# Hybrid attention and gated-MLP block: early gate weights, a second fill bank, and PSUM banks that take a second product

## The chip, the cores and the metric

The kernel runs on one core of a Trainium2 chip. Its time is device microseconds of one execution, the median of several runs. Beside the runs there is one profiled execution with a trace of every engine: PE (TensorE), DVE (VectorE), ACT (ScalarE), POOL (GpSimd) and the queues that issue transfers (SP).

## The reference, cut to what matters

```python
h = rmsnorm(x, norm_gain)                                   # x: 1024 tokens x 1024
q, k, v, gate_a, u_in, v_in, gate_b, g_merge = split(h @ w_in)
attn = block_attention(rope(norm(q)), rope(norm(k)), v) * silu(gate_a)   # 8 q heads, 2 kv heads, 64 wide
y_a  = attn @ w_proj_attn                                   # 512 -> 1024
vv   = layernorm(gelu(v_in))
gm   = gelu(u_in) * (W_s vv + b) * silu(gate_b)             # mixing inside 128-token chunks
y_b  = gm @ w_proj_gmlp                                     # 512 -> 1024
g    = sigmoid(g_merge + b_merge)                           # 1024 tokens x 2 branches x 1024
y    = g[..., 0, :] * y_a + g[..., 1, :] * y_b
out  = rmsnorm(x + y @ w_out, final_gain)
```

Everything is float32. `g_merge` is the widest product: 1024 tokens by 1024 inputs by 2048 outputs.

## The kernel before, in words

Each float32 operand of a matmul is split into a high and a low part (`split`, `split16`), and each product runs as three matmuls: high by high, high by low, low by high (`mm3`). ACT makes the high part, and DVE mostly the low one. The work stands on chip transposed, with channels on the partitions and tokens along the free axis, in halves of 512 tokens.

The program runs through these stages:

- projections of k, v and q (0 to about 138 us);
- attention (about 138 to 437 us). `scores` makes a block of 128 queries by 1024 keys and its softmax, a transposing DMA turns the result, and `mix` multiplies it by v. Between the blocks run the "fills": the projections of u_in, gate_a and gate_b, each a 512 by 512 block of 24 matmuls (`z_mm`) named u20, u21, ga00 and so on;
- `proj_b` makes y_b in eight steps yb0 to yb7 (389 to 447 us). Between them `x_chunk` makes the operands of the gates on DVE and ACT (`make_forms`, the tiles named xf);
- eight gate pairs g0 to g7 (`pair`), with four pairs of y_a products between them (`proj_pair`, named y00 to y03), 456 to 653 us. Each goes through `seven`, which multiplies two 2 x 2 block matrices with seven products instead of eight, and adds the products up on DVE. The products are called 11, 21, T2, T3, T1, 22 and T4; each is 12 matmuls for a gate and 6 for y_a;
- the output projection (`out_mm`, 653 to 735 us) and the final norm.

For a gate pair `pair_weights` loads two weight tiles (`graw`), squares them on ACT for a scale (`gsq`, written to a throw-away tile in the mix's PSUM bank), sums over the partitions with a small matmul (`usg`, in the fill bank), makes the scale with DVE and POOL (`scg`, lines 671 to 675), and forms three sums of weights (`sums`: s1, s2 and a new a21). `pair` then splits each of the seven weights with that scale (`split16`, lines 680 and 681; `wg011` is the weight of product 11 of g0). `MORDER` is the order in which the program writes the gate stage down.

Two kinds of storage matter for the change. PSUM has eight banks of 128 x 512 float32: three tiles `S` of two banks each, one bank `o` (the mix, and the squares' throw-away output) and one bank `z` (the fills and `usg`). In SBUF the tag `t2` has four buffers of 128 x 512. From these come the weight sums s1 and s2 of each gate, the copy `p1` of product 11, the sums `ps` of y_a, and the work tiles of the fills.

The order on each engine is not the one in which the code is written: the program is built with a scheduler that reorders all of it by its own estimate of a timeline. Each engine then works its queue strictly in order, with semaphore waits where a tile is needed or has to come free. A wait goes by tile, so that for a two-bank tile of PSUM it does not tell its banks apart.

Of the kernel before, what the change touches and what calls it, by code (L numbers as in the profile page):

```python
# [12 lines left out]
AF = mybir.ActivationFunctionType  # L13
# [17 lines left out]
def hybrid_block_kernel(  # L31
# [11 lines left out]
    act, dve, pool, pe = nc.scalar, nc.vector, nc.gpsimd, nc.tensor  # L43
# [27 lines left out]
    def ps_s(name):  # L71
        return ps.tile([P, 1024], F32, tag="S", bufs=3, name=name)
# [10 lines left out]
    def H(h):  # L83
        return slice(512 * h, 512 * h + 512)

    def C(c):
        return slice(128 * c, 128 * c + 128)
# [80 lines left out]
        nc.sync.dma_start(out=xn, in_=x[C(tt), :])  # L168
        act.activation(xn, xn, AF.Square, accum_out=ssx[:, tt:tt + 1])

    def mm3(o, ah, al, bh, bl, start, stop):
        pe.matmul(o, ah, bh, start=start, stop=False)  # L172
        pe.matmul(o, ah, bl, start=False, stop=False)  # L173
        pe.matmul(o, al, bh, start=False, stop=stop)  # L174

    kvs = [ps_s(f"kv{b}") for b in range(2)]
    kvb = [s[:, H(h)] for s in kvs for h in range(2)]
    for i in range(4):
        for j in range(2):
            dt = 2 * i + j  # L180
# [4 lines left out]
            raw = load_x(dt)  # L185
# [6 lines left out]
            for tt in range(NT):  # L192
                o = kvb[tt // 2][:, 256 * (tt % 2):256 * (tt % 2) + 256]
# [50 lines left out]
    bmh = const([P, 16], "bmh")  # L244
# [10 lines left out]
    for h in range(2):  # L255
        raw = sb.tile([P, 512], F32, tag="wraw", bufs=4, name=f"wspr{h}")
# [177 lines left out]
    for t2k in range(4):  # L434
# [5 lines left out]
        for v in range(2):  # L440
            for half in range(2):
                dst = kT[64 * half:64 * half + 64, 2 * v:2 * v + 2, 256 * t2k:256 * t2k + 256]
# [54 lines left out]
        dve.scalar_tensor_tensor(out=t, in0=t, scalar=1.0, in1=w, op0=ALU.add, op1=ALU.mult)  # L497
        return t

    FB = (ps_z,)  # L500
    nfill = []

    def fill_bank(name):
# [181 lines left out]

    def seven(name, n, w, B, c, weights):

        def product(key, raw):
            hi, lo = weights(key, raw)
            bank = ps_s(f"{name}{key}")[:, H(0)]  # L690
            for j in range(n):
                mm3(bank, hi[:, C(j)], lo[:, C(j)], *B[key][j], j == 0, j == n - 1)
            return bank

        def add(dst, bank, other):
            dve.tensor_tensor(out=dst, in0=bank, in1=other, op=ALU.add)

        a11, a12, a21, a22, s1, s2 = w
        p1 = t2(f"p1{name}")
        act.copy(p1, product("11", a11))  # L700
        add(c[0][0], product("21", a12), p1)
        add(c[0][1], product("T2", s2), p1)
        dve.tensor_tensor(out=s2, in0=a12, in1=s2, op=ALU.subtract)
        add(c[1][0], product("T3", a21), c[0][1])
        o = product("T1", s1)
        add(c[1][1], o, c[1][0])
        add(c[0][1], o, c[0][1])
        add(c[0][1], product("22", s2), c[0][1])
        yield
        add(c[1][0], product("T4", a22), c[1][0])  # L710
        yield

    def sums(a11, a12, a21, a22, s1, s2):
# [19 lines left out]
    XLO = (dve, dve)  # L733
    XCS = (0, 1, 3, 5)
    EARLY = 2
    MORDER = "w0 g0 w1 g1 w2 A a0 g2 w3 g3 w4 a1 g4 w5 g5 w6 a2 g6 w7 a3 o g7"

    gk = []

# [12 lines left out]
    def load_chunk(j):  # L752
        for dt in (j, j + 4):
            xraw[dt] = t4(XT[j], f"xraw{dt}")
            nc.sync.dma_start(out=xraw[dt], in_=xT[C(dt), :])

    def x_chunk(j):
        q = {}
        for r in range(2):
            dt = j + 4 * r  # L760
            for h in range(2):
                t = q[r, h] = xraw[dt][:, None, H(h)]
                dve.scalar_tensor_tensor(out=xraw[dt][:, H(h)], in0=xraw[dt][:, H(h)], scalar=gs[:, dt:dt + 1],
                                         in1=rB[:, H(h)], op0=ALU.mult, op1=ALU.mult)

        def xf_tile(key, i):
            if not xfn:
                tag = XFT.pop(0)
                if tag == "ptr":
                    t = sb.tile([P, 4, 2, 1, 512], F16, tag="ptr", bufs=2, name=f"xf{key}{j}")  # L770
                else:
                    t = t4(tag, f"xf{key}{j}", F16, (P, 2048)).rearrange("p (n f k t) -> p n f k t", n=2, f=2, k=1)
                xfn.extend(t[:, n] for n in range(t.shape[1]))
            t = xfn.pop(0)
            return t[:, 0], t[:, 1]

        make_forms(q, 1, xf_tile, XB, XSUB, XHI, XLO)

    for j in range(2):
        load_chunk(j)  # L780
    for dt in range(8):
        proj_b(dt)
        if dt in XCS:
            j = XCS.index(dt)
            x_chunk(j)
            if j + 2 < 4:
                load_chunk(j + 2)

    def halves_of(t):
        return [t[:, H(0)], t[:, H(1)]]  # L790

    def proj_pair(i, b, G, dst):
        r0, r1 = load_w(W_PROJ + 2 * i, b), load_w(W_PROJ + 2 * i + 1, b)
        s12 = t2(f"ps{b}{i}")
        w = sums(r0[:, 0:256], r0[:, 256:512], r1[:, 0:256], r1[:, 256:512], s12[:, 0:256], s12[:, 256:512])
        count = [0]

        def weights(key, raw):
            t = sb.tile([P, 2, 256], F32R, tag="wh", bufs=WHB, name=f"wp{b}{i}{key}")
            split(t[:, 0], t[:, 1], raw, act, WPL[count[0] % len(WPL)])  # L800
            count[0] += 1
            return t[:, 0], t[:, 1]

        for _ in seven(f"y{b}{i}", 2, w, G, [halves_of(d) for d in dst], weights):
            pass

    def pair_weights(dt):
        t = t8("qT", 4, f"graw{dt}", F32)
        nc.sync.dma_start(out=t[:, 0, :], in_=wall[W_TR + 20 + dt])
        nc.sync.dma_start(out=t[:, 1, :], in_=wall[W_TR + 12 + dt])  # L810
        a21, a22, a11, a12 = (t[:, k, H(h)] for k in range(2) for h in range(2))
        ss = small(f"gss{dt}", 4)
        for i, t in enumerate((a21, a22, a11, a12)):
            act.activation(junk(f"gsq{dt}{i}"), t, AF.Square, accum_out=ss[:, i:i + 1])
        sc = unit_scale(ss, 4, f"g{dt}")
        return sums(a11, a12, a21, a22, t2(f"s1{dt}"), t2(f"s2{dt}")), sc

    def pair(dt, w, sc):
        def weights(key, raw):
            t = sb.tile([P, 2, 512], F16, tag="wl", bufs=3, name=f"wg{dt}{key}")  # L820
            split16(t[:, 0], t[:, 1], raw, sc, GPW)
            return t[:, 0], t[:, 1]

        ga, gb = (t4(GGT.pop(0), f"g{k}{dt}") for k in "ab")
        it = seven(f"g{dt}", 4, w, XB, [halves_of(ga), halves_of(gb)], weights)
        next(it)
        act.activation(ga, ga, AF.Tanh, bias=bmh[:, dt:dt + 1], scale=sc[:, 1:2])
        next(it)
        act.activation(gb, gb, AF.Tanh, bias=bmh[:, 8 + dt:9 + dt], scale=sc[:, 1:2])
        return ga, gb  # L830

    GGT = GGTAGS.split() * 16
# [4 lines left out]
        dve.tensor_tensor(out=ys[dt], in0=ys[dt], in1=ga, op=ALU.add)  # L837

    gates, GA, pws, yas = {}, {}, {}, {}
    yhl, who = {}, []  # L840

    wor, who4 = [], []
# [39 lines left out]
    for step in MORDER.split():  # L882
        i = int(step[1:] or 0)
# [149 lines left out]
```

## Time and profile before

| what | value |
|---|---|
| runs | 746.56, 747.24, 745.75 us (median 746.56) |
| profiled execution, own time | 744.79 us |
| its span, first to last instruction | 743.0 us |
| mean granted TensorE clock | 0.988 |
| busy: PE, DVE, ACT, POOL | 712.1, 596.4, 446.8, 97.2 us |

The profiled execution is 1.77 us under the median, and its own time is 1.79 us longer than its span. Times of day below, such as 456 us, count from the start of that span. A row of a timeline gives start, duration, engine, line, operation, output<-inputs, and in square brackets the idle time ahead of it with what ended that. Durations of pipelined instructions overlap, so the cost of one in a dense stretch is the distance between two starts. In a table by stretch the columns are the stretch and its length, and then the busy time (with the number of instructions) of PE, weight load, DVE, ACT and POOL, the granted clock, the share of the DMA engines and GB/s.

### The profile page before, as it was taken

Reading aid. Unit: us, or ns where it says so; the run is one execution under the profiler, and the core shown is the slowest. Engines: PE = TensorE matmul, PEld = TensorE weight load, DVE = VectorE, ACT = ScalarE, POOL = GpSimd, SP = SyncE. Lnnn points to the kernel's source line nnn. Section 1 sums busy time; section 2 is a strip of 40 time slices with the busy share of each in tenths; the row PEclk is TensorE's granted clock in tenths of the full one; section 3 lists DMA queues with packets and bytes.
Section 4 is the critical chain, followed back from the end, with each engine's and each line's share of the span. In section 5 each row is a group of like instructions: output and inputs, shape, how many; then the busy total and the mean of one; then the engine's idle time right before and its main releaser. Section 6 shows DMA issues by size and latency. Waiting matters only on the chain.

```text
span 743.0 us, 9814 instructions
## 1 busy us (share of the span) xinstructions
PE 712.1 (96%) x3561; PEld 530.1 (71%) x3561; DVE 596.4 (80%) x931; ACT 446.8 (60%) x775; POOL 97.2 (13%) x77
## 2 busy tenths in 40 slices
PE   8999999988999999999999995999999998999995
PEld 8978888766778888888878882455464555588884
DVE  5568988789798999988899999899888899934223
ACT  6646664676788898768787488555474446611101
POOL 0010242142121321232200002000000000000000
PEclk9999999989999999999999998999999999999998
DMA  8831301083769897898999800130031006241111
GB/s 309 301 100 36 114 15 42 1 142 78 136 128 181 166 179 142 162 177 157 166 234 323 183 16 1 56 128 15 18 125 57 0 1 231 109 142 68 46 58 56
DMA packets 152609, 85.47 MB, mean 115 GB/s; under 512 B 135408, under 2 KB 136048, under 8 KB 152560
## 3 DMA queue, kind: packets, MB, share of 16 engines
q1 hardware_dynamic: 152272, 84.56, 45.7%
q8 instruction: 28, 0.46, 0.3%
q10 hardware_dynamic: 288, 0.28, 0.1%
q14 instruction: 21, 0.17, 0.1%
HBM read 47.07 MB, written 4.19 MB: 69 GB/s over the span
## 4 chain that ended last, share of the span: by engine, by line
PE 81%; DVE 9%; DMA 4%; ACT 2%; issue 2%; POOL 1%; SPq 0%; POOLq 0%; DVEq 0%; ACTq 0%
PE o L575 6%; PE out L174 4%; PE out L173 4%; PE out L172 4%; DMA T<-p 3%; PE s L550 3%; PE s L551 3%; PE g L172 3%; PE g L174 3%; PE g L173 3%; PE q L172 2%; PE q L174 2%; PE v L172 2%; PE q L173 2%; PE v L173 2%; PE v L174 2%
## 5 line engine op out<-in xcount | busy, mean ns | idle before, releaser
L564 DVE SCALAR_TENSOR_TENSOR p<-P,ri,p 128x1024 f16<-128x1024 f32 x64 | 88.9, 1393 | 14.7 <-ACT p L563 14.3
L557 ACT ACTIVATE P<-s,nm 128x1024 f32<-128x1024 f32 x64 | 71.4, 1116 | 23.0 <-DVE nm L553 11.5
L553 DVE TENSOR_REDUCE nm<-s 128x1 f32<-128x1024 f32 x64 | 77.8, 1215 | 5.7 <-PE s L551 5.4
L563 ACT ACTIVATE p<-P,ri 128x1024 f16<-128x1024 f32 x64 | 72.8, 1143 | 14.7 <-DMA T<-p 11.3
L575 PE MATMUL o<-T,vS 128*128 128x256 f16 x512 | 61.8, 273 | 2.1 <-DMA T<-p 2.1
L575 PEld LDWEIGHTS <-vS 128*128 128x128 f16 x512 | 47.4, 98 | 16.0 <-issue 6.9
L550 PE MATMUL s<-kT,qT 128*128 128x512 f32 x128 | 53.0, 414 | 1.3 <-ACT P L557 1.3
L116 POOL TENSOR_TENSOR wl<-wraw,wh 128x512 fp32r<-128x512 f32 x24 | 36.0, 1504 | 111.6 <-ACT wh L110 96.2
L551 PE MATMUL s<-kT,qT 128*128 128x512 f32 x128 | 50.5, 395 | 0.0
L909 ACT ACTIVATE sq<-xr 128x1024 f32<-128x1024 f32 x7 | 7.4, 1061 | 61.5 <-DVE xr L963 61.5
L963 DVE TENSOR_TENSOR xr<-out,xr 128x1024 f32<-128x1024 f32 x7 | 8.6, 1225 | 44.0 <-PE out L174 43.9
L673 POOL TENSOR_TENSOR scg<-scg,mhalf 128x1 f32<-128x1 f32 x8 | 9.8, 1219 | 221.6 <-DVE scg L672 221.6
L110 ACT CAST wh<-wraw 128x512 fp32r<-128x512 f32 x35 | 21.5, 614 | 17.5 <-PE yb L173 7.5
L488 PE MATMUL ga<-xh,wh 128*128 128x512 f32 x64 | 26.5, 414 | 3.8 <-DVE uw L511 3.4
L550 PEld LDWEIGHTS s<-kT,qT 128*128 128x128 f32 x128 | 24.1, 188 | 6.7 <-ACT P L557 1.9
L551 PEld LDWEIGHTS s<-kT,qT 128*128 128x128 f32 x128 | 24.1, 188 | 4.9 <-issue 0.2
L488 PE MATMUL u<-xh,wh 128*128 128x512 f32 x64 | 25.6, 399 | 0.7 <-DVE ga01w L494 0.7
L490 PE MATMUL ga<-xh,wl 128*128 128x512 f32 x64 | 26.1, 407 | 0.0
L489 PE MATMUL ga<-xl,wh 128*128 128x512 f32 x64 | 26.0, 406 | 0.0
L680 ACT ACTIVATE wg<-graw,scg 128x512 f16<-128x512 f32 x16 | 11.4, 721 | 24.2 <-PE g L174 12.8
L172 PE MATMUL v<-nh,xh 128*128 128x512 f32 x64 | 25.5, 398 | 0.0
L174 PE MATMUL yb<-gmh,wl 128*128 128x512 f32 x64 | 25.5, 398 | 0.0
(557 smaller groups left out, 2158.5 us busy)
## 6 DMA issues: line engine op xcount, KB each, us to landing
wraw<-in_wall_dram SPq DMA_DIRECT2D x59, 256.0 KB, 3.2
graw<-in_wall_dram SPq DMA_DIRECT2D x16, 512.0 KB, 4.4
xraw<-in_xT_dram SPq DMA_DIRECT2D x15, 512.0 KB, 7.3
xn<-in_x_dram SPq DMA_DIRECT2D x8, 512.0 KB, 7.6
wor<-in_wall_dram SPq DMA_DIRECT2D x8, 512.0 KB, 4.9
xr<-in_x_dram SPq DMA_DIRECT2D x8, 512.0 KB, 5.1
out_dram<-xr SPq DMA_DIRECT2D x7, 512.0 KB, 2.6
T<-p SPq DMA_TRANSPOSE x64, 4.6
```

The costliest lines, as they stand in the source:

```text
L116: eng_lo.tensor_tensor(out=lo, in0=raw, in1=hi if hi.dtype == F16 else hi.bitcast(F32), op=ALU.subtract)
L172: pe.matmul(o, ah, bh, start=start, stop=False)
L173: pe.matmul(o, ah, bl, start=False, stop=False)
L174: pe.matmul(o, al, bh, start=False, stop=stop)
L488: pe.matmul(o, wh[:, C(dt % 4)], xh[dt][:, H(h)], start=(dt == 0), stop=False)
L550: pe.matmul(sp[:, H(hf)], qs, kT[:, 2 * v, H(hf)], start=True, stop=False)
L551: pe.matmul(sp[:, H(hf)], qs, kT[:, 2 * v + 1, H(hf)], start=False, stop=True)
L553: dve.tensor_reduce(out=nm, in_=sp, axis=AX.X, op=ALU.max, negate=True)
L557: act.activation(Pt, sp, AF.Exp, bias=nm, accum_out=rsum)
L563: act.activation(hi, Pt, AF.Copy, scale=ri)
L564: dve.scalar_tensor_tensor(out=lo, in0=Pt, scalar=ri, in1=hi, op0=ALU.mult, op1=ALU.subtract)
L575: pe.matmul(ot[:, 0:256], vS[:, kt, v, :], T[:, :, 8 * p + kt, :], start=(kt == 0 and p == 0), stop=(kt == 7 and p == 1))
```

## The change

`seven` takes two two-bank tiles, `xy` and `wz`, for its whole run, instead of a tile for each product. Their four banks are X, Y, W and Z. Product 21 is accumulated on top of 11 in X, T4 on top of T3 in W, and 22 on top of T1 in Z, so five additions on DVE do what seven did. The block that ends in X is read by ACT straight out of PSUM: by the tanh of the gate, which now comes in three pieces instead of two, or by a new copy in `proj_pair`. The products are written in the order 11, T2, T3, 21, T1, T4, 22. The second fill, u21, gets the bank `o` instead of `z`. The weights and scales of g0 and g1 are written into the loop of `proj_b`, after its steps 3 and 5, and leave `MORDER`. The argument `skip_group_check` concerns a check of the builder and emits nothing.

```diff
-    FB = (ps_z,)
+    FB = (ps_z, ps_o)
...
     def seven(name, n, w, B, c, weights):
-        def product(key, raw):
+        xy, wz = ps_s(f"{name}xy"), ps_s(f"{name}wz")
+        X, Y, W, Z = xy[:, H(0)], xy[:, H(1)], wz[:, H(0)], wz[:, H(1)]
+
+        def product(bank, key, raw, first=True):
             hi, lo = weights(key, raw)
-            bank = ps_s(f"{name}{key}")[:, H(0)]
             for j in range(n):
-                mm3(bank, hi[:, C(j)], lo[:, C(j)], *B[key][j], j == 0, j == n - 1)
-            return bank
+                mm3(bank, hi[:, C(j)], lo[:, C(j)], *B[key][j], first and j == 0, j == n - 1, not first)
...
-        act.copy(p1, product("11", a11))
-        add(c[0][0], product("21", a12), p1)
-        add(c[0][1], product("T2", s2), p1)
+        product(X, "11", a11)
+        act.copy(p1, X)
+        product(Y, "T2", s2)
+        add(c[0][1], Y, p1)
         dve.tensor_tensor(out=s2, in0=a12, in1=s2, op=ALU.subtract)
-        add(c[1][0], product("T3", a21), c[0][1])
-        o = product("T1", s1)
-        add(c[1][1], o, c[1][0])
-        add(c[0][1], o, c[0][1])
-        add(c[0][1], product("22", s2), c[0][1])
+        product(W, "T3", a21)
+        add(c[1][0], W, c[0][1])
+        product(X, "21", a12, False)
+        yield X
+        product(Z, "T1", s1)
+        add(c[1][1], Z, c[1][0])
+        product(W, "T4", a22, False)
+        add(c[1][0], W, c[0][1])
         yield
-        add(c[1][0], product("T4", a22), c[1][0])
+        product(Z, "22", s2, False)
+        add(c[0][1], Z, c[0][1])
         yield
...
-    MORDER = "w0 g0 w1 g1 w2 A a0 g2 w3 g3 w4 a1 g4 w5 g5 w6 a2 g6 w7 a3 o g7"
+    MORDER = "g0 g1 w2 A a0 g2 w3 g3 w4 a1 g4 w5 g5 w6 a2 g6 w7 a3 o g7"
...
-        for _ in seven(f"y{b}{i}", 2, w, G, [halves_of(d) for d in dst], weights):
-            pass
+        for bank in seven(f"y{b}{i}", 2, w, G, [halves_of(d) for d in dst], weights):
+            if bank is not None:
+                act.copy(dst[0][:, H(0)], bank)
...
+        ba, bb = bmh[:, dt:dt + 1], bmh[:, 8 + dt:9 + dt]
+        act.activation(ga[:, H(0)], next(it), AF.Tanh, bias=ba, scale=sc[:, 1:2])
         next(it)
-        act.activation(ga, ga, AF.Tanh, bias=bmh[:, dt:dt + 1], scale=sc[:, 1:2])
+        act.activation(gb, gb, AF.Tanh, bias=bb, scale=sc[:, 1:2])
         next(it)
-        act.activation(gb, gb, AF.Tanh, bias=bmh[:, 8 + dt:9 + dt], scale=sc[:, 1:2])
+        act.activation(ga[:, H(1)], ga[:, H(1)], AF.Tanh, bias=ba, scale=sc[:, 1:2])
...
     for dt in range(8):
         proj_b(dt)
...
+        if dt in (3, 5):
+            pws[dt // 4] = pair_weights(dt // 4)
```

The lines of the changed kernel are numbered a little higher: z_mm's 488 to 490 become 489 to 491, mm3's 172 to 174 become 173 to 175, the split's 680 and 681 become 681 and 682, the addition in `seven` 696 becomes 699, and its copy to `p1` 700 becomes 704.

The three places below show the order on the engines, with what each row waits for in square brackets.

The first is PE at the start of attention, where the first fills run (qtp30 and qtp31 are the two halves of q for token block 3, transposed on PE). Before:

```order
L349 MATMUL qtp30_1308<-identr_71,qs3_1305 128x128 [waits DVE_49,PE_49,Activation_49]
L488 MATMUL u21_1525<-xh0_93,wh160_1482 128x512 [waits DVE_49]
L489 MATMUL u21_1525<-xl0_94,wh160_1482 128x512
...
L490 MATMUL u21_1525<-xh7_334,wl161_1489 128x512
L349 MATMUL qtp31_1315<-identr_71,qs3_1305 128x128 [waits PE_49,Activation_49]
L488 MATMUL ga00_1889<-xh0_93,wh100_1879 128x512 [waits DVE_49]
L489 MATMUL ga00_1889<-xl0_94,wh100_1879 128x512
```

and after:

```order
L350 MATMUL qtp30_1308<-identr_71,qs3_1305 128x128 [waits DVE_49,PE_49,Activation_49]
L489 MATMUL ga00_1889<-xh0_93,wh100_1879 128x512 [waits DVE_49]
L490 MATMUL ga00_1889<-xl0_94,wh100_1879 128x512
...
L350 MATMUL qtp31_1315<-identr_71,qs3_1305 128x128 [waits PE_49,Activation_49]
L350 MATMUL qtp31_1315<-identr_71,qs3_1305 128x128 x3
L490 MATMUL u21_1525<-xl0_94,wh160_1482 128x512
...
L350 MATMUL qtp4_1576<-identr_71,qs4_1573 128x128 [waits DVE_49]
```

Half of ga00 now stands ahead of u21, in the bank `z`, and u21 follows in the bank `o`; before, ga00 stood behind all of u21 and waited for DVE to read u21 out of the same bank.

The second place is the first gate pair, g0. On PE before (the last matmul of a product and the first of the next; the weight loads between are left out):

```order
L174 MATMUL g0T3_4661<-xfT33_4503,wg0T3_4658 128x512
...
L172 MATMUL g0T1_4678<-xf110_4250,wg0T1_4675 128x512 [waits DVE_49]
...
L172 MATMUL g022_4696<-xf110_4250,wg022_4693 128x512 [waits DVE_49]
...
L172 MATMUL g0T4_4714<-xfT40_4268,wg0T4_4711 128x512 [waits DVE_49]
...
L172 MATMUL g111_4760<-xf110_4250,wg111_4757 128x512 [waits DVE_49]
```

and after:

```order
L175 MATMUL g0wz_4631<-xfT33_4528,wg0T3_4666 128x512
...
L173 MATMUL g0xy_4630<-xfT20_4262,wg0T2_4649 128x512 [waits Activation_49]
...
L175 MATMUL g0xy_4630<-xfT33_4528,wg0T2_4649 128x512
...
L173 MATMUL g0xy_4630<-xfT20_4262,wg021_4682 128x512 [waits DVE_49]
...
L173 MATMUL g0wz_4631<-xf110_4250,wg0T1_4698 128x512 [waits DVE_49]
...
L173 MATMUL g0wz_4631<-xfT40_4268,wg0T4_4714 128x512 [waits DVE_49]
```

Before, three `S` tiles take turns, and each of these waits is for the addition that reads the product three places earlier (T1 waits for the one that reads 21, and so on). The products now stand in the order 11 with T3, T2, 21, T1, T4. T2 (tile g0xy) waits for the copy of 11 on ACT, 21 for DVE's addition that reads T2 in the same tile, and T4 for the addition that reads T1 in the tile g0wz. That copy stands on ACT, after:

```order
L681 ACTIVATE wg021_4682<-graw0_4425,scg0_4439 128x512 [waits PE_49,Activation_49]
L110 CAST gk_4912<-gat2_3889 128x1024 [waits DVE_49]
L110 CAST gfT30_4908<-gat0_1919 128x1024 [waits DVE_49]
L110 CAST xfT31_4321<-xraw5_4212 128x512 [waits DVE_49]
L681 ACTIVATE wg0T1_4698<-s10_4445,scg0_4439 128x512 [waits PE_49]
L704 COPY p1g0_4632<-g0xy_4630 128x512 [waits DVE_49]
```

It has moved behind the split of the weight of T1 and waits for DVE: its buffer of `t2` is that of s10, whose last reader is the low part of that weight. In the changed order s10, s20, s11 and s21 hold all four buffers of `t2` at that time; before, s21 was made after p1g0. The low part stands on DVE, after:

```order
L682 SCALAR_TENSOR_TENSOR wg021_4682<-graw0_4425,scg0_4439,wg021_4682 128x512 [waits Activation_49]
L676 TENSOR_SCALAR scg1_4553<-scg1_4553,gsc_440 128x1 [waits DVE_49]
L116 TENSOR_TENSOR gk_4912<-gat2_3889,gk_4912 128x1024 [waits Activation_49]
L116 TENSOR_TENSOR xfT31_4321<-xraw5_4212,xfT31_4321 128x512 [waits Activation_49]
L682 SCALAR_TENSOR_TENSOR wg0T1_4698<-s10_4445,scg0_4439,wg0T1_4698 128x512 [waits Activation_49]
L116 TENSOR_TENSOR gfT31_4909<-gat0_1919,gfT30_4908 128x1024 [waits DVE_49]
L699 TENSOR_TENSOR ga0_4628<-g0xy_4630,p1g0_4632 128x512 [waits PE_49,Activation_49]
L699 TENSOR_TENSOR gb0_4629<-g0wz_4631,ga0_4628 128x512 [waits DVE_49]
```

Its place, three rows ahead of the addition that reads T2, is the one from which p1g0, and so T2, now starts.

The third place is DVE at the end of the last pair, g7, after:

```order
L699 TENSOR_TENSOR gb7_6028<-g7wz_6030,gb7_6028 128x512 [waits PE_49]
L872 TENSOR_TENSOR wo51_6172<-wor5_6010,wo50_6171 128x1024 [waits DMAHW4_49,PE_49]
L872 TENSOR_TENSOR wo61_6179<-wor6_6012,wo60_6178 128x1024 [waits DMAHW5_49,DVE_49,Activation_49]
L888 SCALAR_TENSOR_TENSOR yhl4_6168<-y47_4201,yhl4_6168 128x1024 [waits Activation_49]
L699 TENSOR_TENSOR gb7_6028<-g7wz_6030,ga7_6027 128x512 [waits PE_49]
L837 SCALAR_TENSOR_TENSOR y47_4201<-gb7_6028,y47_4201 128x1024 [waits Activation_49]
L872 TENSOR_TENSOR wo71_6187<-wor7_6014,wo70_6186 128x1024 [waits DMAHW6_49,PE_49]
L888 SCALAR_TENSOR_TENSOR yhl5_6175<-y47_4201,yhl5_6175 128x1024 [waits Activation_49]
L699 TENSOR_TENSOR ga7_6027<-g7wz_6030,ga7_6027 128x512 [waits PE_49]
```

The last row reads product 22 out of g7wz and so frees that tile. On PE the output tile out2 takes it, directly behind product 22:

```order
L173 MATMUL g7wz_6030<-xfT40_4268,wg7T4_6113 128x512 [waits DVE_49]
...
L173 MATMUL g7wz_6030<-xf110_4250,wg722_6130 128x512 [waits DVE_49]
...
L175 MATMUL g7wz_6030<-xfT13_4521,wg722_6130 128x512
L173 MATMUL out2_6214<-who_6016,yhl0_6019 128x512 [waits DVE_49]
L174 MATMUL out2_6214<-who_6016,yhl0_6019 128x512
```

So between T4's addition and the one that lets out2 start stand a merge (y47, line 837), a low part of an output weight (wo71) and a low part of y (yhl5). Before, three `S` tiles came free one after the other, and out0, out1 and out2 followed g7's products in three separate tiles.

More of the change, by code (lines that the diff above doesn't have):

```diff
@@ L169, in add_square, with mm3 @@
         act.activation(xn, xn, AF.Square, accum_out=ssx[:, tt:tt + 1])
[L171 to L174, printed above, removed]
+    def mm3(o, ah, al, bh, bl, start, stop, more=False):
+        pe.matmul(o, ah, bh, start=start, stop=False, skip_group_check=more)
+        pe.matmul(o, ah, bl, start=False, stop=False, skip_group_check=more)
+        pe.matmul(o, al, bh, start=False, stop=stop, skip_group_check=more)
     kvs = [ps_s(f"kv{b}") for b in range(2)]
@@ L777, in x_chunk @@
         make_forms(q, 1, xf_tile, XB, XSUB, XHI, XLO)
[L779 to L787, printed above, removed]
     def halves_of(t):
@@ L839, in hybrid_block_kernel @@
     gates, GA, pws, yas = {}, {}, {}, {}
+    for j in range(2):
+        load_chunk(j)
+    for dt in range(8):
+        proj_b(dt)
+        if dt in XCS:
+            j = XCS.index(dt)
+            x_chunk(j)
+            if j + 2 < 4:
+                load_chunk(j + 2)
+        if dt in (3, 5):
+            pws[dt // 4] = pair_weights(dt // 4)
     yhl, who = {}, []
```

## Prediction

> **What bounds the kernel now.** I read the page's first two parts, then the table of busy time by stretch, and then PE's timeline wherever that table shows it short of full.
>
> ```profile
> PE 712.1 (96%) x3561; PEld 530.1 (71%) x3561; DVE 596.4 (80%) x931; ACT 446.8 (60%) x775; POOL 97.2 (13%) x77
> ...
> 140.00:160.00 20.00, 16.60 (x76) 13.38 (x75) 18.43 (x25) 15.92 (x33) 7.32 (x4) 0.89 0.41 79
> 160.00:200.00 40.00, 35.90 (x197) 28.65 (x196) 32.89 (x50) 25.87 (x53) 8.46 (x5) 0.97 0.62 106
> ...
> 440.00:470.00 30.00, 20.76 (x86) 11.25 (x84) 29.05 (x50) 22.91 (x44) 6.08 (x2) 0.89 0.00 1
> 470.00:500.00 30.00, 30.00 (x141) 15.35 (x140) 27.11 (x47) 18.09 (x29) 0.93 (x1) 1.00 0.30 104
> 500.00:550.00 50.00, 50.00 (x232) 27.89 (x231) 43.01 (x77) 27.09 (x53) 1.10 (x2) 1.00 0.17 59
> ...
> 600.00:630.00 30.00, 27.82 (x126) 15.83 (x125) 28.19 (x46) 15.18 (x22) 0.55 (x1) 1.00 0.33 122
> ```
>
> PE is the bound: 712.1 of 743.0 us. From 470 on it is full, except for 2.2 us between 600 and 630, although DVE is busy 86 to 94% there. So the gate stage has no PE idle time to win, and each microsecond for which a gate matmul waits in the changed kernel is added to the end. What can be won stands in 140 to 200 and 440 to 470. In the latter DVE is busy 29.05 of 30 us: there DVE's queue sets the time, and the clock falls to 0.89.
>
> **The first fills.** The first place of the change is this hole:
>
> ```profile
> 152.90 0.46 PE L349 MATMUL qtp<-identr,qs 128*128 128x128 f32 x4
> 156.76 0.80 PE L488 MATMUL ga<-xh,wh 128*128 128x512 f32 x1 [3.40 <-DVE uw L511]
> 157.35 0.63 PE L489 MATMUL ga<-xl,wh 128*128 128x512 f32 x1
> 157.78 0.63 PE L490 MATMUL ga<-xh,wl 128*128 128x512 f32 x1
> ...
> 162.66 0.40 PE L490 MATMUL ga<-xh,wl 128*128 128x512 f32 x1
> 162.90 0.39 PE L488 MATMUL ga<-xh,wh 128*128 128x512 f32 x1
> ```
>
> ga00 waits 3.40 us for DVE to read u21 out of the only fill bank. Then the matmuls start 0.43 us apart instead of 0.24 for twelve of them (156.76 to 162.05), another 2.4 us. With the second bank, half of ga00 and all of u21 follow each other without that wait. What is left is that qtp31 and u21 wait for ACT's copies of q and that qtp4 waits for DVE; I estimate two idle spells of about 1.1 us, too short to slow the clock as the 3.40 us did. Gain 5.8 - 2.3 = 3.5 us. Bounds: 5.8 if nothing new waits, and 0 if the softmax chain takes it back: PE is idle 4.1 us in 160 to 200 too, with DMA engines 0.62 busy, so that there the chain of scores, softmax and transposing transfers may set the pace and not the fills. I take 3.5, as the slow clock goes in any case.
>
> **The early weights.** This is the second hole, between yb7 and g0:
>
> ```profile
> 446.90 0.40 PE L174 MATMUL yb<-gmh,wl 128*128 128x512 f32 x1
> 448.43 0.39 PE L669 MATMUL usg<-gss,mhalf 128*128 128x4 f32 x2 [1.14 <-ACT gsq L814]
> 454.48 0.59 PE L669 MATMUL usg<-gss,mhalf 128*128 128x4 f32 x2 [5.67 <-ACT gsq L814]
> 455.90 0.61 PE L172 MATMUL g<-xf,wg 128*128 128x512 f16 x1 [0.82 <-ACT wg L680]
> 456.30 0.63 PE L173 MATMUL g<-xf,wg 128*128 128x512 f16 x1
> ...
> 459.34 0.38 PE L173 MATMUL g<-xfT,wg 128*128 128x512 f16 x1
> 459.55 0.38 PE L174 MATMUL g<-xfT,wg 128*128 128x512 f16 x1
> ```
>
> g0 starts 8.8 us after yb7's last slot, and its first matmuls run 0.42 us apart instead of 0.22, up to 459.34: 1.7 us more. Written earlier, the chain gsq, usg, scg could fill that hole. But in the changed order both usg still stand behind all of yb7 on PE, directly ahead of g0, and the reduce behind them stands in the same place on DVE: gsq writes its throw-away output into the mix's bank, which is free only when the last mix has been read. Only s11, s21 and g1's a21 have moved ahead on DVE, three operations of 0.60 us each (from one DVE start to the next). I cost the early weights themselves at nothing: what they add to DVE ahead of g0 ends inside the wait that comes next, and they close no hole.
>
> **The copy of 11 in g0.** That early s21 has a second effect. s10, s20, s11 and s21 hold all four buffers of t2, so p1g0 waits for the last reader of s10, the low part of T1's weight, and T2 waits for p1g0, since it writes the other half of the tile. Before:
>
> ```profile
> 461.26 0.59 ACT L700 COPY p1g<-g 128x512 f32<-128x512 f32 x1
> 466.78 0.74 DVE L681 SCALAR_TENSOR_TENSOR wg0T<-graw,scg,wg0T 128x512 f16<-128x512 f32 x1
> 467.58 0.39 PE L174 MATMUL g0T<-xf,wg0T 128*128 128x512 f16 x1 [1.61 <-DVE wg0T L681]
> 469.25 0.74 DVE L681 SCALAR_TENSOR_TENSOR wg0T<-s,scg,wg0T 128x512 f16<-128x512 f32 x1
> 477.31 0.38 PE L174 MATMUL g0T<-xf,wg0T 128*128 128x512 f16 x1
> 477.73 0.69 DVE L696 TENSOR_TENSOR gb<-g0T,gb 128x512 f32<-128x512 f32 x1 [0.23 <-PE g0T L174]
> ```
>
> Product 11 ended, and ACT copied it at 461.26 into a buffer of its own. After, 11 and T3 (24 matmuls from 455.9, 0.22 us each, and 1.7 us of slow clock) end at about 463 to 464.5. The low part of T1's weight ran at 469.25 (the row whose input is s). Ahead of it DVE now has s21 more (0.60) and the addition of 21 less (0.60), so I leave it there; with the copy of 0.59 us behind it, T2 starts at about 470. PE has nothing else in its queue: some 6 us idle.
>
> From T2 on, five products' worth are left of the seven, 5 x 2.59 = 13.0 us (12 matmuls x 0.216; 467.58 to 477.31 are 45 of them). Two additions now stand on the path, since 21 follows T2 and T4 follows T1 directly. The price of one is seen in the last two rows: PE's last slot ends at 477.52, the addition starts at 477.73, the next operation on DVE could start 0.60 later, and PE restarts 0.06 us after DVE is done (467.58 against 466.78 + 0.74): 0.96 us with rounding, if DVE is free. So the seventh product ends at 470 + 13.0 + 1.9 = 484.9, against 477.5: +7.4. The idle 6 us are longer than the 3.40 us which slowed the clock, so again 0 to 2.4 us; I take half of the 1.7 seen at g0: +0.8. Together **+8.2**, bounds +1.4 (p1g0 is not late at all) and +9.8. I take the upper part, because the rows of DVE up to there are the ones of before, at 29.05 busy of 30.
>
> [...]
>
> **The other pairs.** Each later pair has the same two additions on PE's path, unless other products stand between. In g1, g3 and g5 y_a's products do (1.39 us a product), so I cost these at 0; uncovered they would be 1.9 each. In g2 and g4 nothing covers them: T1 to T4 0.96, and at T2 to 21 DVE comes late, with merges ahead of the addition:
>
> ```profile
> 505.42 1.22 DVE L835 SCALAR_TENSOR_TENSOR ga<-ga,ya 128x1024 f32<-128x1024 f32 x1
> 506.55 0.68 DVE L696 TENSOR_TENSOR ya<-y00T,ya 128x512 f32<-128x512 f32 x1
> 507.15 1.21 DVE L837 TENSOR_TENSOR y<-y,ga 128x1024 f32<-128x1024 f32 x1
> ```
>
> In the changed queue a merge of 1.13, a weight's low part, another 1.14 and s23 of 0.60 stand between the last y_a addition and that of T2. That makes 0.96 to 2.2, and I take 1.55: 2.5 a pair, **+5.0** for two (3.8 to 6.4). g6 has one y_a product of 1.39 at T2 to 21 and two at T1 to T4: **+0.4** (0 to 0.8).
>
> **DVE's smaller load.** 24 additions of 0.60 us go, 14.4 us, and each gate's tanh is three pieces instead of two on ACT (60% busy), with four copies for y_a. PE, not DVE, is the bound there, so I cost this at 0; it is why I keep the additions near their free price.
>
> **The end.** Two things change:
>
> ```profile
> 624.25 0.50 PE L174 MATMUL y<-gf,wp 128*128 128x512 f32 x1 [0.63 <-DVE wp L116]
> 627.46 0.50 PE L174 MATMUL y03T<-gfT,wp03T 128*128 128x512 f32 x1 [1.55 <-DVE wp03T L116]
> 649.23 1.22 DVE L859 TENSOR_TENSOR wo<-wor,wo 128x1024 fp32r<-128x1024 f32 x1
> 649.35 1.25 ACT L829 ACTIVATE gb<-gb,bmh,scg 128x1024 f32<-128x1024 f32 x1 [1.47 <-DVE gb L696]
> 651.50 1.22 DVE L836 SCALAR_TENSOR_TENSOR y<-gb,y 128x1024 f32<-128x1024 f32 x1
> 653.77 1.22 DVE L875 SCALAR_TENSOR_TENSOR yhl<-y,yhl 128x1024 fp32r<-128x1024 f32 x1
> ```
>
> y03's products are now spread among those of g6 and g7, so the waits of 0.63 and 1.55 go: -2.2. In g7, 22 waits 0.96 for the addition of T4. Then out2 needs g7wz, and its release stands on DVE behind a merge that waits for ACT: from the end of T4 0.8 (addition), 1.25 (tanh), and 1.13 + 1.13 + 1.13 + 0.60 on DVE, or 6.1 us; product 22 ends 3.55 us after T4. That leaves 2.6, so **+1.4** in all. Bounds: -1.2 if out2's wait is covered, +3.6 if the first two waits come back elsewhere.
>
> **Sum.** -3.5 + 8.2 + 5.0 + 0.4 + 1.4 = +11.5 us. On the profiled execution that is 744.79 + 11.5 = 756.3; the median of the runs stands 1.8 above it, so **758.1 us**. All lower bounds give -5.8 + 1.4 + 3.8 + 0 - 1.2 = -1.8 (744.8), all upper ones 0 + 9.8 + 6.4 + 0.8 + 3.6 = +20.6 (767.2).
>
> **Rivals.**
>
> - Faster: the early weights do close the hole ahead of g0. If the eight gsq ran before the last steps of y_b, most of the 8.8 us, the 1.7 of slow clock and the 1.6 at 467.58 would go, about -11. p1g0 would not be late, and the additions (1.9 + 5.0 + 0.4 + 1.4) stay: -11 - 3.5 + 8.7 = -5.8, 740.8 us. It decides as soon as g0 starts before about 451. For it speaks that the weights are asked for two to four steps of y_b earlier; against it, that gsq's output goes to the mix's bank and the queues of PE and DVE have the chain where it was.
> - About the same: p1g0 is hardly late and all terms lie at their lower ends, 744.8. DVE's smaller load speaks for it; the 29.05 of 30 us against, as none of the saved additions but one lies ahead of that wait.
> - Much slower: the softmax chain takes the first term back, and the clock falls after each new wait: 767.
>
> **Chances.** Forecast 0.62, with a range of its own of 750 to 764; hole closed 0.14; lower ends 0.12, split between faster and same by the 744.8 against 746.56; much slower 0.12. About 0.2% (1.5 us) is what a measurement of this kernel can tell from no change: faster 0.19, same 0.06, slower 0.75. Leaving out most of the closed hole below and some of the upper tail, 743 to 766 holds 8 in 10.
>
> **What the changed profile would show.** Right: PE idle before the second product tile of g0, released by ACT's p1g; waits of about 1 us released by DVE's addition, twice each in g0, g2 and g4; no 3.40 us before ga; a wait of some 2.6 us at out2; usg still behind yb7. Wrong: usg among the yb matmuls; additions that end before PE needs them; the stretch 160 to 200 shorter of PE work than before; or y_a's products waiting for DVE in the odd pairs.

## The result, and the profile after

The changed kernel takes 766.19 us (median of 4 runs, 763.95 to 768.62), the kernel before 746.16 in the same comparison. The ratio is 1.028, with a 95% interval of 1.0258 to 1.0301: 20 us slower. The forecast was slower by 11.5 us, at 758.1, in a range of its own of 750 to 764.

The profiled execution took 765.91 us. Its page, part 1, and the table by stretch (columns as before):

```profile
PE 721.2 (94%) x3561; PEld 529.4 (69%) x3561; DVE 584.2 (76%) x907; ACT 449.7 (59%) x787; POOL 95.0 (12%) x77
...
140.00:160.00 20.00, 18.73 (x101) 15.08 (x100) 18.66 (x27) 16.15 (x34) 6.49 (x4) 1.00 0.40 75
160.00:200.00 40.00, 37.56 (x211) 29.71 (x209) 37.46 (x54) 29.06 (x60) 13.77 (x8) 1.00 0.69 138
440.00:470.00 30.00, 17.45 (x60) 8.68 (x59) 26.78 (x44) 19.27 (x37) 2.54 (x2) 0.78 0.06 20
470.00:500.00 30.00, 28.20 (x128) 13.64 (x127) 20.52 (x35) 16.36 (x29) 0.55 (x1) 0.99 0.13 43
500.00:550.00 50.00, 47.33 (x211) 24.03 (x211) 35.96 (x62) 24.30 (x47) 1.10 (x2) 0.97 0.15 54
550.00:600.00 50.00, 47.33 (x211) 24.00 (x210) 36.20 (x62) 23.79 (x46) 1.10 (x2) 0.97 0.16 57
```

DVE has its 24 additions less (907 instructions instead of 931, 584 us instead of 596), and PE is fuller in the first fills (18.73 instead of 16.60 us of the 20 from 140 on) and no longer full in the gate stage: it has 5.3 us of idle time between 500 and 600, where it had none. The list of PE's waits (tile waited with, line, released by, total, times, longest) names them:

```profile
PE usg L670 <- ACT gsq L813: 6.6, 2, 6.4
PE s L551 <- ACT P L558: 4.6, 6, 1.2
PE g0xy L173 <- ACT p1g L704: 3.9, 1, 3.9
PE out L173 <- DVE ga L699: 2.7, 1, 2.7
PE g7wz L173 <- DVE gb L699: 2.4, 1, 2.4
PE g2xy L173 <- DVE ga L699: 1.9, 1, 1.9
PE g4xy L173 <- DVE ga L699: 1.9, 1, 1.9
...
PE g2wz L173 <- DVE gb L699: 0.8, 1, 0.8
```

On PE's timeline the same waits stand with what follows them:

```profile
466.69 0.38 PE L173 MATMUL g0xy<-xfT,wg0T 128*128 128x512 f16 x1 [3.90 <-ACT p1g L704]
...
471.98 0.38 PE L173 MATMUL g0xy<-xfT,wg 128*128 128x512 f16 x1 [0.85 <-DVE ga L699]
...
478.68 0.38 PE L173 MATMUL g0wz<-xfT,wg0T 128*128 128x512 f16 x1 [0.78 <-DVE gb L699]
...
521.87 0.57 PE L173 MATMUL g2xy<-xfT,wg 128*128 128x512 f16 x1 [1.89 <-DVE ga L699]
522.23 0.63 PE L174 MATMUL g2xy<-xfT,wg 128*128 128x512 f16 x1
...
572.89 0.39 PE L173 MATMUL g4xy<-xfT,wg 128*128 128x512 f16 x1 [1.89 <-DVE ga L699]
...
669.21 0.38 PE L173 MATMUL g7wz<-xf,wg 128*128 128x512 f16 x1 [2.43 <-DVE gb L699]
...
674.61 0.50 PE L173 MATMUL out<-who,yhl 128*128 128x512 f32 x1 [2.66 <-DVE ga L699]
```

T2 of g0 waits for the copy of 11; then 21 and T4 each wait for an addition; the same pair of waits stands in g2 and g4; T4's addition holds product 22 in g7 (2.43), and out2 waits 2.66. Behind 521.87 the matmuls stand about 0.43 us apart instead of 0.216 for eight steps: the clock has slowed. The granted clock from 521.90 to 525.40 is 0.51, and 1.00 in the 2.5 us behind it. Behind four of these waits (p1g0, g2, g4, out2) such a slow spell costs 1.62 to 1.66 us each; another stands at the start of g0 (2.68, against 1.71 before).

The start of the first score matmul differs between profiles (135.5 to 138.9 us; 135.47 and 138.50 in two executions of the changed kernel), so I count from it. The table gives the last slot of y_b, and then the points at which whole pairs are done, from rows of both timelines:

| point | before | after | later by | of this, in the stage that ends here |
|---|---|---|---|---|
| last matmul of y_b | 311.16 | 309.11 | -2.05 | -2.05 |
| g0 and product 11 of g1 done | 344.37 | 350.97 | +6.60 | +8.65 |
| g2 and product 11 of g3 done | 390.71 | 401.98 | +11.27 | +4.67 |
| g4 and product 11 of g5 done | 436.89 | 453.00 | +16.11 | +4.84 |
| last matmul | 599.16 | 620.56 | +21.40 | +5.29 |

Before, these points lie at the starts of the next product (480.11, 526.45 and 572.63); after, at 486.44, 537.45 and 588.47. The span grew by 21.1 us.

### The profile page after: what moved, and what is told of

It reads as the page before. It is cut to its first block, busy times and chain, and to the rows that moved or that the text cites. A ratio compares the mean times of both kernels' runs of the same rounds, so it can differ in the third digit from the quotient of the medians.

```text
span 764.1 us, 9766 instructions
## 1 busy us (share of the span) xinstructions
PE 721.2 (94%) x3561; PEld 529.4 (69%) x3561; DVE 584.2 (76%) x907; ACT 449.7 (59%) x787; POOL 95.0 (12%) x77
## 4 chain that ended last, share of the span: by engine, by line
PE 66%; DVE 17%; ACT 6%; DMA 6%; issue 3%; POOL 1%; SPq 1%; POOLq 0%; ACTq 0%; DVEq 0%
DMA T<-p 5%; PE out L173 4%; PE out L174 4%; PE out L175 4%; DVE p L565 4%; ACT p L564 3%; DVE nm L554 2%; PE o L576 2%; PE q L173 2%; PE v L174 2%; PE q L175 2%; PE q L174 2%; PE v L173 2%; PE v L175 2%; PE s L551 2%
## 5 line engine op out<-in xcount | busy, mean ns | idle before, releaser
L565 DVE SCALAR_TENSOR_TENSOR p<-P,ri,p 128x1024 f16<-128x1024 f32 x64 | 85.6, 1344 | 17.8 <-ACT p L564 17.3
L116 POOL TENSOR_TENSOR wl<-wraw,wh 128x512 fp32r<-128x512 f32 x24 | 38.9, 1625 | 106.6 <-ACT wh L110 61.4
L674 POOL TENSOR_TENSOR scg<-scg,mhalf 128x1 f32<-128x1 f32 x8 | 5.8, 729 | 237.2 <-DVE scg L673 237.2
L489 PE MATMUL gb<-xh,wh 128*128 128x512 f32 x64 | 25.5, 399 | 0.1
L175 PE MATMUL v<-nh,xl 128*128 128x512 f32 x64 | 25.4, 396 | 0.0
L173 PE MATMUL q<-nh,xh 128*128 128x512 f32 x64 | 25.2, 394 | 0.0
```

What stands on the lines that cost most here:

```text
L116: eng_lo.tensor_tensor(out=lo, in0=raw, in1=hi if hi.dtype == F16 else hi.bitcast(F32), op=ALU.subtract)
L173: pe.matmul(o, ah, bh, start=start, stop=False, skip_group_check=more)
L175: pe.matmul(o, al, bh, start=False, stop=stop, skip_group_check=more)
L489: pe.matmul(o, wh[:, C(dt % 4)], xh[dt][:, H(h)], start=(dt == 0), stop=False)
L565: dve.scalar_tensor_tensor(out=lo, in0=Pt, scalar=ri, in1=hi, op0=ALU.mult, op1=ALU.subtract)
```

## The experiments

The theory: the time went into PE waits which arise because a wait goes by the two-bank tile, and into a slow clock behind some of them. Starts of stages named below count from the first score as above.

**One part undone.** Three kernels take one part out of the change; a fourth keeps all parts and pairs the banks otherwise.

```diff
-        xy, wz = ps_s(f"{name}xy"), ps_s(f"{name}wz")
-        X, Y, W, Z = xy[:, H(0)], xy[:, H(1)], wz[:, H(0)], wz[:, H(1)]
+        xz, yw = ps_s(f"{name}xz"), ps_s(f"{name}yw")
+        X, Z, Y, W = xz[:, H(0)], xz[:, H(1)], yw[:, H(0)], yw[:, H(1)]
```

> The changed kernel with one line different: X and Z now share one two-bank tile and Y and W the other, so that products which follow each other mostly write different tiles. Theory A (the time went into PE waits, made because a wait goes by the two-bank tile, plus a slow clock after some of them): the waits of 1.89, 0.78, 2.43 and the slow spells of 1.6 us in g2, g4 and at the end go, the wait for p1g0 stays: about 751 us (748 to 755). Theory B (the second product in a bank, or the pieces read by ACT from PSUM, cost time by themselves): unchanged, 766.

Measured 756.31 us (1.0125, interval 1.0097 to 1.0153): 10 us of the loss are gone with another pairing of the same four banks. Its list of waits:

```profile
...
PE g0xz L173 <- ACT p1g L704: 3.0, 1, 3.0
...
PE g0yw L174 <- DVE xfT L116: 1.6, 1, 1.6
...
PE g2yw L173 <- DVE gb L699: 0.8, 1, 0.8
PE g4yw L173 <- DVE gb L699: 0.8, 1, 0.8
```

The waits of 1.9 in g2 and g4, of 2.4 in g7 and of 2.7 at out2 are gone; the one for p1g0 (now ahead of 21) stays. The scheduler also moved products: in g2, 21 now stands ahead of T2, and part of T1 between T2 and T3. Theory B falls as the account of the whole loss, as the same second products run in the same banks. The 0.78 in g2 and g4, which I had expected to go, stayed, for another reason:

```profile
526.95 0.69 DVE L699 TENSOR_TENSOR gb<-g2yw,ga 128x512 f32<-128x512 f32 x1 [0.20 <-PE g2yw L175]
...
527.70 0.38 PE L173 MATMUL g2yw<-xfT,wg2T 128*128 128x512 f16 x1 [0.78 <-DVE gb L699]
```

Here T4 directly follows T3, on top of which it is accumulated in W, and waits for the addition that reads T3 there. This wait belongs to the second product in a bank, not to the pairing. My 751 was 5 us low: g0 waits another 1.64 for its operands, its spells of slow clock (3.7 us) stay, and g7 waits 1.41 for a weight.

```diff
-    MORDER = "g0 g1 w2 A a0 ...          (weights of g0, g1 in the loop of proj_b)
+    MORDER = "w0 g0 w1 g1 w2 A a0 ...
```

> The changed kernel with the weights of g0 and g1 back in the gate stage's order. Theory A: p1g0 has a buffer of its own again, its wait of 3.90 us and the slow spell of 1.66 behind it go, all else stays: about 761 us (759 to 763). Rival C (the early weights, by their work on DVE and ACT ahead of g0, cause most of the loss): 750 or less.

Measured 761.80 us (1.0202, 1.0174 to 1.0230), as expected, but not by the way expected. p1g0 has its buffer, yet 21 then waits for the addition that stands behind the splits on DVE:

```profile
467.19 0.38 PE L173 MATMUL g0xy<-xfT,wg 128*128 128x512 f16 x1 [3.58 <-DVE ga L699]
...
519.12 0.38 PE L173 MATMUL g2xy<-xfT,wg 128*128 128x512 f16 x1 [1.89 <-DVE ga L699]
519.33 0.38 PE L174 MATMUL g2xy<-xfT,wg 128*128 128x512 f16 x1
```

So the buffer is worth little by itself: DVE's queue holds g0. Of the 4.3 us by which g0 with product 11 of g1 is shorter here, from the end of y_b, 3.4 lie ahead of its first matmul; e9 below shows why. The wait of 1.89 in g2 is there to the hundredth, and this time the clock did not slow behind it (0.21 us from row to row, granted clock 1.00 from 519.10 to 522.50).

```diff
-    FB = (ps_z, ps_o)
+    FB = (ps_z,)
```

> The changed kernel with every fill in the one fill bank again. Theory A: the 2.3 us by which the changed kernel is ahead at the end of y_b are lost: 768.5 us (767 to 770). Rival D (the softmax chain gives the time back whatever the fills do): 766.

Measured 766.44 us (1.0259, 1.0223 to 1.0295): beside the rest of the change the second fill bank is worth nothing that the runs can tell, as rival D said.

```profile
157.26 0.79 PE L489 MATMUL ga<-xh,wh 128*128 128x512 f32 x1 [3.40 <-DVE uw L512]
...
468.90 0.38 PE L173 MATMUL g0xy<-xfT,wg0T 128*128 128x512 f16 x1 [3.02 <-ACT p1g L704]
```

The old hole is back, and y_b ends 2.5 us later than in the changed kernel, but p1g0 is waited for 0.9 us less, and the slow spell behind it is 0.6 us shorter: part of the later start is absorbed by waits that were there anyway. The rest is not settled by this profile, the fastest of the four runs (762.46), in which the clock did not slow in g2 and g4. That out2 waits 0.97 instead of 2.66 is no gain either, as product 22 ahead of it ran at the slow clock here.

```diff
-    (seven with tiles xy and wz, five additions, three pieces of tanh)
+    (seven as before: a tile for each product, seven additions, two tanh)
```

> The changed kernel with the old seven (seven tiles, seven additions) and the old two tanh, but the second fill bank and the early weights. Theory A: the waits in g2, g4 and g7 are gone, the fill bank's 2.3 us stay, and p1g0 still waits for its buffer, which holds back T3 in g0 by some 2 to 4 us with its slow clock: 747 us (744 to 750). Rival C (the early weights cause most): 758 or more.

Measured 747.02 us (1.0024, 1.0002 to 1.0046), as expected: without the new `seven` the loss is gone. The buffer of p1g0 shows, and holds T3 instead of T2:

```profile
468.63 0.38 PE L173 MATMUL g0T<-xf,wg0T 128*128 128x512 f16 x1 [2.71 <-ACT p1g L701]
```

**What holds g0.** Two edits take away what the prediction and its faster rival named, a third joins them.

```diff
-        p1 = t2(f"p1{name}")
+        p1 = c[0][0]                  # first half of the output tile, written last by the tanh
```

> The changed kernel, with the copy of product 11 in the first half of the pair's output tile (free until the last tanh) instead of a buffer of t2. Theory A (wait for the buffer, then for DVE's queue): the wait for p1g0 goes, but 21 now waits for the addition that stands behind the same splits on DVE, about one product later: 762 us (760 to 764). Rival E (the wait for the buffer alone, DVE would be ready): 760 or less, with 21 waiting under 1.5 us.

Measured 757.47 us (1.0170, 1.0149 to 1.0190), 5 us better than I expected.

```profile
470.32 0.38 PE L173 MATMUL g0xy<-xfT,wg 128*128 128x512 f16 x1 [0.86 <-DVE ga L699]
...
478.32 0.55 PE L670 MATMUL usg<-gss,mhalf 128*128 128x4 f32 x2 [2.66 <-ACT gsq L813]
```

21 waits only 0.86, which rival E had asked for, though a small matmul for g2's scale then holds the queue for 2.66. But more moved than the buffer: the scheduler put a y_a product ahead of 21 in g2 and g4, and the two waits of 1.9 are gone. From the first score to the last matmul the kernel is 10.7 us shorter than the changed one, of which 2.0 in g0 and 7.3 in g2 and g4. The kernel therefore does not measure the buffer alone, and does not decide between A and E.

```diff
     def junk(name):
-        return ps_o(name)
+        return ps_z(name)
```

> The changed kernel with the throw-away output of the squares in the fill bank instead of the mix's bank; the small sums of the scale then stand among the matmuls of y_b. Theory A (DVE's queue sets when g0 gets on): g0 starts some 7 us earlier and then waits longer for p1g0, 764 us (762 to 766). Rival F (the chain of the scale in the mix's bank is what holds g0): 759 or less.

Measured 768.80 us (1.0320, 1.0289 to 1.0351). g0 now starts 0.2 us after y_b (311.89 against 311.66) instead of 9.0, and is done later: with product 11 of g1 it takes 4.9 us longer, counted from the first score, of which y_b 2.5.

```profile
455.70 0.61 PE L175 MATMUL g0wz<-xf,wg0T 128*128 128x512 f16 x1 [3.30 <-DVE wg0T L682]
...
457.44 0.59 PE L174 MATMUL g0xy<-xfT,wg 128*128 128x512 f16 x1 [1.13 <-DVE xfT L116]
...
463.32 0.38 PE L174 MATMUL g0wz<-xfT,wg0T 128*128 128x512 f16 x1 [1.78 <-DVE xfT L116]
...
469.34 0.58 PE L173 MATMUL g0xy<-xfT,wg0T 128*128 128x512 f16 x1 [4.13 <-ACT p1g L704]
```

This is the faster rival of the prediction, made true: the chain of the scale is out of the way, the hole closes, and PE waits about as long in several pieces, most of them for DVE's operand splits. DVE is busy 29.76 of the 30 us from 440 to 470 there. Rival F falls: closing the hole alone gains nothing while DVE's queue is full.

```diff
-        X, Y, W, Z = xy[:, H(0)], ...        p1 = t2(...)       junk -> ps_o
+        X, Z, Y, W = xz[:, H(0)], ...        p1 = c[0][0]       junk -> ps_z
```

> The changed kernel with three edits together: X with Z and Y with W in a tile, the copy of 11 in the output tile, and the squares' output in the fill bank. Theory A: no wait is left in g1 to g7 but some of under 1 us; g0 is still held back by DVE's queue: 750 us (747 to 753). Rival F: 744 or less.

Measured 760.27 us (1.0205, 1.0182 to 1.0228), 10 us above my figure and worse than e1. (The lines above show the three edits side by side.)

```profile
521.73 0.38 PE L173 MATMUL g2yw<-xf,wg2T 128*128 128x512 f16 x1 [2.63 <-DVE ga L699]
```

In this order T3 follows T2 directly, both in the tile yw, so T3 waits for T2's addition (2.65 in g0 and g4). In e1 part of T1 stood between. So this pairing helped where the order let products alternate between the tiles, and not where it did not.

**The clock.** The changed kernel, profiled again without an edit:

> The changed kernel once more, for its slow clock: if a wait of 1.89 us always slows the clock, g2 and g4 each show a slow spell of 1.6 us again; if it depends on something that the length of the wait does not decide, as e2 and e3 suggest (the same two waits of 1.89 us and no slow spell), some of them are missing, and the time is shorter by 1.6 us for each.

Measured 768.64 us (2 runs, 769.25 and 768.03). The same two waits, 1.88 us each:

```profile
526.94 0.38 PE L173 MATMUL g2xy<-xfT,wg 128*128 128x512 f16 x1 [1.88 <-DVE ga L699]
527.15 0.38 PE L174 MATMUL g2xy<-xfT,wg 128*128 128x512 f16 x1
...
576.24 0.51 PE L173 MATMUL g4xy<-xfT,wg 128*128 128x512 f16 x1 [1.88 <-DVE ga L699]
576.54 0.63 PE L174 MATMUL g4xy<-xfT,wg 128*128 128x512 f16 x1
```

g2 ran on at full clock (granted 1.00 from 526.90 to 530.40) and g4 did not (0.53 from 576.20 to 579.80), in one execution. The stage of g2 is 1.7 us shorter for it than in the first profile, as expected; the time is not, since y_b ended 1.6 us later in this profile. Over the six profiles that have these two waits (after, e2, e3, e6, e8, e11) five of twelve were followed by a slow spell of 1.6 to 1.7 us. Single waits of 1.61 us (g0 before, at 467.58) and 1.78 us (g0 in e9) were not. The wait of 2.43 in g7 slowed the clock in three of six, that of 2.66 at out2 in three of four (after, e2 and e8, not e5).

**One part alone, on the kernel before.**

```diff
-    FB = (ps_z,)
+    FB = (ps_z, ps_o)
```

> The kernel before with the second fill bank alone. In e4 and e1 y_b ended 1.2 to 1.8 us earlier than before, counted from the first score, and g0 then waits for DVE's queue in part. Theory A (about half of the gain at the fills survives): 745.2 us, 0.1 to 0.2% faster. Rival D (the softmax chain or DVE's queue takes all of it): the time of before within 0.05%.

Measured 742.78 us against 745.92 (0.9967, 0.9954 to 0.9980): 3.1 us faster, more than either theory gave, and faster than both kernels. It is not the fills that keep it: the gain there (the eighth mix ends about 3.2 us earlier) is gone by the twelfth (1.4 us later), and y_b ends at 311.63 against 311.16. But g0 starts at 317.55 instead of 320.16, and 1.8 us of that are left at the last matmul (597.34 against 599.16); the rest of the 3.1 is not in these two profiles.

```profile
447.55 0.28 PE L669 MATMUL usg<-gss,mhalf 128*128 128x4 f32 x2
453.24 0.61 PE L172 MATMUL g<-xf,wg 128*128 128x512 f16 x1 [5.41 <-ACT wg L680]
...
458.16 0.28 PE L669 MATMUL usg<-gss,mhalf 128*128 128x4 f32 x2
```

Before, the small matmul for g1's scale stood ahead of g0's first product in PE's queue and waited 5.67 us for ACT's squares. Here the scheduler has put it in the middle of g0. That is what the rows show; it was not tried by itself. The same turn of the order stands in e2 and e12, the two other kernels that have the second bank and keep the weights in the gate stage: there g0 starts 5.6 us after y_b's last matmul, here 5.9. With the second bank and the early weights (the changed kernel, e1, e4 and e5) it is 9.0 to 9.4 us, and without the second bank (before, e3, e10, e11) 8.7 to 9.4. So what the second bank gives at g0 is lost where the weights are written early.

```diff
+        if dt in (3, 5):
+            pws[dt // 4] = pair_weights(dt // 4)        # and no w0, w1 in MORDER
```

> The kernel before with the early weights of g0 and g1 alone. Theory A: p1g0 waits for its buffer and holds back T3 by some 2.7 us instead of the 1.6 us that T2 waited before, nothing else changes: 747.3 us (746.3 to 748.5). Rival C (they close part of the hole ahead of g0): 745 or less.

Measured 748.29 us (1.0034, 1.0014 to 1.0054): 2.4 us slower. g0 starts at 319.61, only 0.5 us earlier than before, so rival C falls here too: the early weights close nothing. T3 waited only 0.18 us for p1g0 (the 1.6 us of before were T3's, not T2's); the operand wait in g0 is 1.01 us, and the clock lost 2.2 us at the start of g0 instead of 1.7. Of the time from the first score to the last matmul nothing is lost in this profile (599.34 against 599.16). Its first score starts 2.1 us later (137.87 against 135.74), and two executions of the changed kernel differ there by 3 us. So the profile does not show that the 2.4 us come from the early weights.

```diff
     (seven, proj_pair and pair of the change; FB and MORDER of the kernel before)
```

> The kernel before with the rewritten seven alone (two tiles, second products, five additions, the tanh in pieces). Theory A: nearly the whole loss is here: 762.5 us (761 to 766), with the same waits in g2, g4, g7 and at out2. Rival G (the loss needs the parts together): 755 or less.

Measured 765.95 us (1.0268, 1.0252 to 1.0285): the rewritten `seven` alone is the whole loss.

```profile
...
PE g0xy L173 <- DVE ga L699: 4.4, 1, 4.4
...
PE g7wz L173 <- DVE gb L699: 2.4, 1, 2.4
...
PE g2xy L173 <- DVE ga L699: 1.9, 1, 1.9
PE g4xy L173 <- DVE ga L699: 1.9, 1, 1.9
```

The waits of g2, g4 and g7 are those of the changed kernel; in g0 it is 21 that waits, for 4.40, and out2 waits 1.45 instead of 2.66. By the medians, three parts alone give -3.1 + 2.4 + 20.0 = +19.3 us, all together +20. The parts are not independent even so: the second bank is worth 3.1 us alone and nothing in e3, and the early weights cost 2.4 alone and 4.4 beside the rest of the change (766.19 against e2's 761.80).

The last kernel is the change again, with two edits:

```diff
-        X, Y, W, Z = xy[:, H(0)], ...        weights of g0, g1 in the loop of proj_b
+        X, Z, Y, W = xz[:, H(0)], ...        MORDER = "w0 g0 w1 g1 ...
```

> The changed kernel with X and Z, Y and W paired, and the weights of g0 and g1 back in the gate stage. Theory A: e1's waits in g1 to g7 are as small as there, and in g0 p1g0 has a buffer, but 21 still waits for DVE's queue by some 2 us: 752 us (750 to 754). If p1g0's buffer were all that held g0 in e1: 748.

Measured 751.41 us (1.0077, 1.0056 to 1.0098). The time is as expected, the wait is not: 21 of g0 waits 0.25 us at most, and operands are waited for there, 0.84 and 1.50. With the other pairing and the weights where they were, 5.5 us over the kernel before remain. Against e9, which has the old `seven` with the same fill banks and weights, the new one costs 8.6 us even so. No version of the new `seven` that ran here beats the old one.

## Why the prediction was right or wrong, point by point

| term | forecast | measured (from the first score) |
|---|---|---|
| first fills | -3.5 | -2.05 at the end of y_b |
| g0 | +8.2 | +8.65 |
| g2 and g4 | +5.0 | +9.5 |
| g6, g7, end | +1.8 | +5.3 |
| sum | +11.5 | +21.4 |

The mechanism was right: every wait that it named is in the profile, released by the instruction that it named, e4 and e11 show that the loss comes with the new `seven`, and e1 that half of it goes with another pairing of its banks. Sizes were off: of the 9.9 us between forecast and measurement 4.5 lie in g2 and g4, 3.5 at the end, 1.45 in the first fills and 0.45 in g0.

**The other pairs.** The step that failed most is the 2.5 us a pair taken for g2 and g4, which measured 4.67 and 4.84. The wait at 21 measured 1.89, where I took the middle of 0.96 and 2.2 although I had counted DVE's queue ahead of it (two merges, a split and s23); and I priced a slow clock behind the 6 us wait of g0 only, which put the one behind the waits of g2 and g4 at nothing. It came behind waits of 1.89 too, for 1.62 and 1.65 us: 1.89 + 0.78 + 1.6, and some tenths around them, make the 4.67.

**The end.** Product 22 of g7 was priced at a free DVE (0.96). DVE had two low parts of output weights and one of y ahead of T4's addition:

```profile
664.88 2.54 DVE L872 TENSOR_TENSOR wo<-wor,wo 128x1024 fp32r<-128x1024 f32 x2 [4.45 <-PE g7wz L175]
667.34 1.22 DVE L888 SCALAR_TENSOR_TENSOR yhl<-y,yhl 128x1024 fp32r<-128x1024 f32 x1
668.47 0.68 DVE L699 TENSOR_TENSOR gb<-g7wz,ga 128x512 f32<-128x512 f32 x1
```

These rows stood in the changed order, directly ahead of that addition, and the first of them had itself waited 4.45 us for a product of g7: DVE was not loaded there, its queue was held. The wait was 2.43, and 1.66 us of slow clock followed out2's 2.66 (forecast 2.6).

**The first fills.** The hole went and the clock stayed up, as forecast (granted 1.00 from 140 to 200 us, where the longest wait is 1.23 us; before, 0.50 from 156.80 to 162.00, behind the 3.40 us), but six waits for the softmax (4.6 us in all; 4.1 to 5.2 in every kernel with the second bank, 1.3 to 1.6 in e3, e10 and e11) took part of it back. The bound that named this was right, the value chosen was not, and by e3 nothing that the runs can tell of it reaches the end in the changed kernel.

**g0.** +8.65 against +8.2, but that the two are so near is luck, as the split inside is another. I had left the low part of T1's weight at 469.25 and T2 at about 470. That low part ran sooner, and T2 started at 466.69:

```profile
465.28 0.74 DVE L682 SCALAR_TENSOR_TENSOR wg0T<-s,scg,wg0T 128x512 f16<-128x512 f32 x1
```

So p1g0 was waited for 3.9 us, not 6, while slow spells took 2.6 us more of g0 than before (2.68 + 1.66 - 1.71), and not 0.8. That the early weights close no hole was right, but not that they cost nothing: beside the second bank they keep it open (e9). And e6 shows that not the bank of the squares alone made the hole, but DVE's work ahead of g0.

Covered as forecast: the odd pairs have no wait of 0.25 us or more at their additions, and the waits of 0.63 and 1.55 in y03 are gone. Of the rivals, "much slower" came nearest, 767, by the two ways that it named, each in part: 2.05 us of the first term were left at the end of y_b, and the clock fell behind four of the new waits and not behind each.

Taken together, the waits of 1.88 to 2.66 us that the section on the clock counts were followed by a slow spell in eleven of 22 cases (five of twelve in g2 and g4, three of six in g7, three of four at out2); in g2 and g4 it lost 1.6 to 1.7 us.

## What to carry to other kernels

Fewer additions on an engine that is not the bound bought nothing here (24 less on DVE, 584 us busy instead of 596, and 20 us slower). Putting a second result into the other half of a tile tied the producer to what reads the first half (T2 of g0 waited 3.90 us for the copy of 11, 21 of g2 1.89 us for T2's addition), and putting it on top of the first tied it to the first one's reader (0.78 us at T4 of g2 in e1): before packing PSUM banks, write down for each product which read it must wait for and how many products lie between. Price such a wait from the queue of the engine that does the read, row by row, and not from the engine's load; and where PE is full, add what the clock may lose behind the wait (1.6 to 1.7 us behind five of the twelve waits of 1.88 and 1.89 us here). Where two engines share a gap, moving the chain that seems to cause it may only show the other one, as in e6.

## What the runs showed of the hardware that I had not expected

The granted clock fell behind PE waits of only 1.88 us, in five of twelve cases, and not at all behind the single waits of 0.78, 1.61 and 1.78 us named above. In e12 it fell behind the 1.50 us, which had the waits of 0.84 and 0.25 us close ahead of it. The same wait at the same place slowed it in one execution and not in the next. Each slow spell in g2 and g4 lost 1.6 to 1.7 us over eight or nine matmuls, at a granted clock of about 0.5 (0.51 in g2 and 0.53 in g4 of the changed kernel). What decides it is open.
